# Odd mixer reordered: the first head pair ahead of v, pools among the later pairs, the output product to match; score products on all 128 rows

## The chip, the cores and the metric

One core of one Trainium2 chip runs the whole program. The metric is the device time of one execution in microseconds (us); several executions are timed and their median is given. The profile is one further execution taken by the hardware profiler. TensorE is written PE, its weight loads PEld, VectorE DVE, ScalarE ACT, GpSimd POOL and SyncE SP.

## The reference, cut to what matters

A trunk of two layers on 512 tokens of width 1024 in float32. Each layer is a SwiGLU block, a mixer and a SwiGLU block. The first (even) layer mixes with two recurrences; the second (odd) layer with attention and pooling. Only the odd mixer is touched:

```python
proj = h @ odd_w_in                       # 1024 -> q, k, v, u of 512 columns each
q, k, v, u = jnp.split(proj, [512, 1024, 1536], axis=-1)
y_c = _chunk_band_attention(q, k, v, ...) # 8 heads of 64; q and k normalized per head
y_d = _multiscale_pool(u, pool_w, scale)  # 4 groups of 128 channels, windows 2, 4, 8, 16
mixed = jnp.concatenate([y_c, y_d], axis=-1) @ odd_w_out
x = x + mixed
...
scores = einsum('bclhd,bckhd->bhclk', q, k) * 64**-0.5 + bias      # then softmax, then @ v
pooled = trailing_mean(u, w) - u;  y_d = (pooled @ pool_w[g]) * scale
```

## The kernel before, in words

The program is written down in one pass by a Python class that keeps an estimate of each engine's clock. Each engine executes its instructions in the order in which they were written, so the order is fixed at build time. There is a main stream of PE products; between its groups of products, generators ("threads": a norm, a pooling group, an attention block) emit their next instructions when the estimate says that an engine could start on them. Since one helper records every operation, all instructions carry one line in the profile (L203); they are told apart by the names of their tiles.

All large products are made in three passes for precision: an operand is split into an upper and a lower part (`fp32r`), and upper x upper, upper x lower and lower x upper are added up in PSUM. So a product of one 128 x 128 weight block with 128 x 512 of activations is a group of three PE instructions of 512 columns (`ps<-hg,whl`, or `ps<-whl,hg` for v). A weight unit (`raw`, 128 x 1024, 512 KB) is loaded by SP's DMA queue, and split into `whl` by an ACT cast and a DVE subtraction; the units that a table `BY_DMA` names (of `wod` those at places 8 to 11, of `wodo` the first four) get the lower part by two ACT operations and an adding DMA that POOL issues. Outside of the SwiGLU blocks three `whl` tiles rotate.

The odd mixer (function `odd`) runs in this order:

- v for all tokens: four units `wv`, each 24 instructions of PE, into four banks of PSUM; ACT scales them into `vt` (a `hg` tile).
- twelve units `wod` of 24 instructions each, in the order k0 q0 k1 q1 k2 q2 k3 q3 pool3 pool2 pool1 pool0, where k and q are of a pair of heads (128 columns). DVE multiplies each result by the rows' norm factors (`rsB`) on its way out of PSUM.
- after each q, a thread `qk_norm`: squares (`sqk`, ACT), their sums per head by 64 products of 2 columns in all (`ps<-hm,sqk`), a Newton square root on DVE (`rqv`, `rqt`, `rqy`), the factors spread by PE (`ps<-ident,rx`), and the split into `ks` (upper part over lower part, 128 rows), `qs` (upper part twice) and `ql` (lower part of q).
- attention blocks (`attn`, pair t, block qi of 128 queries), two at a time in the order of pairs: scores, on DVE bias and maximum (`s<-ps,rqy,strip`, `st<-s`), exponential on ACT, reciprocal and scaling on DVE, transposes on PE (`ps<-ident,s`), ACT copies (`pT`), products with v (`ps<-pT,hg`, each head into 64 rows of PSUM). The pair's result is split into a `hg` tile when its four blocks are done.
- pooling groups (`pool_g`): doubling sums on DVE (`pl`, `plo`), a product with `pw`, ACT and DVE to split it.
- the output product: eight units `wodo`, four for each half of the columns, in the order OUT_ORDER = 2, 3, 0, 1, where unit kp needs mixed tiles 2 kp and 2 kp + 1: kp 0 pairs 0 and 1, kp 1 pairs 2 and 3, kp 2 pools 0 and 1, kp 3 pools 2 and 3. The next SwiGLU block follows.

The score of a head is two PE instructions of N = 128 (qi + 1) columns: one that contracts all 128 rows of `qs` and `ks`, and one that contracts 64 rows, `ql` with the upper part in `ks`:

```python
nc.tensor.matmul(out=pss[hh][:, 0:N], lhsT=qs[:, hh, qc], rhs=ks[:, hh, 0:N], start=True, stop=False)
nc.tensor.matmul(out=pss[hh][:, 0:N], lhsT=ql[rows[hh], qc], rhs=ks[rows[hh], hh, 0:N], start=False, stop=True)
```

The functions that the diff touches:

Of the kernel before, what the change touches and what calls it, by code (L numbers as in the profile page):

```python
# [32 lines left out]
for _i in range(4):  # L33
    ODD_ORDER += [("k", _i, 512 + P * _i), ("q", _i, P * _i)]
ODD_ORDER += [("pool", _i, 1536 + P * _i) for _i in (3, 2, 1, 0)]
PRM = 2048
OUT_ORDER = [2, 3, 0, 1]
# FFN: quads of four weight units (gate and up of two column tiles) in groups; a group's down products run
# between the pairs of the next group
# [4 lines left out]
# tiles: of all phases, and more of them in the FFNs  # L44
# [42 lines left out]
def unit_plan(stages):  # L87
    plan = []
    for s in stages:
        if s == "even":  # L90
            plan += [("wev", n) for n in range(len(EVEN_ORDER))] + [("wglu", j) for j in range(2)]
            plan += [("wevo", cg, kp) for cg in range(2) for kp in OUT_ORDER]
        elif s == "odd":
            plan += [("wv", kp) for kp in range(4)] + [("wod", n) for n in range(len(ODD_ORDER))]
            plan += [("wodo", cg, kp) for cg in range(2) for kp in OUT_ORDER]
        elif s[0] == "f":
            plan += [k for k in ffn_items(int(s[1])) if k[0] != "blocks"]
    return plan
# [8 lines left out]
class Clock:  # L107
    """An estimate, while the program is written down, of when each engine gets to what it has been given."""
# [106 lines left out]
class Ring:  # L215
    """Tiles of one kind, counted: taken when they are made and given back with their last reader."""
# [31 lines left out]
class Builder:  # L248
# [31 lines left out]
    # generators that emit their parts in turn with the main stream of products  # L280
# [34 lines left out]
    # waits in a generator until an engine could start on these operands without holding up others  # L315
# [14 lines left out]
    # counted tiles: a place is taken before the tile is made and left with its last reader  # L330
# [23 lines left out]
    # banks of PSUM  # L354
# [78 lines left out]
    # products that nothing reads keep the tensor engine's clock up while it waits  # L433
# [6 lines left out]
    # the mixers' small parameters  # L440
# [33 lines left out]
    # weight units come in the order of the plan, loaded and split ahead of their products  # L474
# [95 lines left out]
    # the lower part as minus the upper one plus the weights themselves, added by the DMA  # L570
# [44 lines left out]
    # RMS norm: x times the gains, split, goes into the products, and the rows' factors come after them  # L615
# [46 lines left out]
    # what the norm left; its factors may come later  # L662
# [11 lines left out]
    # two units, so that there is work while the last parts of h come in  # L674
# [34 lines left out]
    # what waits for the norm's factors  # L709
# [7 lines left out]
    # one unit of an output product into four banks; the last one finishes the banks one by one  # L717
# [23 lines left out]
    # the FFN, its gate and up products in seven block products for eight (Strassen's scheme in Winograd's form):  # L741
    # the blocks are two column tiles by two halves of D (weights) and two halves of D by two of the tokens
# [83 lines left out]
    # the last output products begin: what they finish goes on to the next norm  # L826
# [23 lines left out]
    # x, normalized, as float32 (from the split parts when x has gone on)  # L850
# [15 lines left out]
    # sums of blocks of the normalized x  # L866
    def blocks(self, h, gi, late):
# [5 lines left out]
        # the last ones stay until they can go in place of h, the others are made again  # L873
# [29 lines left out]
        # the normalized x itself takes the place of what the unnormalized products read  # L903
# [29 lines left out]
    def pair(self, w, tag):  # L933
# [6 lines left out]
        # of two products in a bank, the one that is read first comes last: one engine at a time in a bank  # L940
# [30 lines left out]
    # up * silu(gate), split; how much of it is done: 1 the silu, 2 the product too  # L971
# [18 lines left out]
    # accurate functions on small tiles  # L990
# [51 lines left out]
    # parameters of the S5 mixer, per eighth of its groups, into DRAM scratch  # L1042
    def s5_prepare(self, pool):
# [100 lines left out]
        # powers of the unit phase: E, E^2, ... E^32  # L1144
# [6 lines left out]
        # the same for pairs of groups, one in each half of the partitions  # L1151
# [6 lines left out]
        # G, K and T0  # L1158
        def gains_of_outputs(e):
# [14 lines left out]
            # K and T0, a group in each quarter of the partitions  # L1174
# [23 lines left out]
        # B  # L1198
# [25 lines left out]
        # rotation tables and decay, for half of the groups  # L1224
# [96 lines left out]
    def s5_quarter(self, q, ys):  # L1321
# [13 lines left out]
        # 2*gelu(y), split  # L1335
# [82 lines left out]
    # SSD  # L1418
# [81 lines left out]
    # o <- 2*o*sigmoid(2*o), by a silu as long as the activation engine has its table, or else by a tanh  # L1500
# [241 lines left out]
    def qk_norm(self, t, kq):  # L1742
# [32 lines left out]
        # per head: key parts and query parts, one over the other, for the exact products  # L1775
# [5 lines left out]
        ql = p.tile([P, S], F32R, tag="ql", name=self.n("ql"), bufs=2)  # L1781
        half = [slice(0, 64), slice(64, 128)]
        for hh in range(2):
            me, other = half[hh], half[1 - hh]
            yield from self.on("ACT", qf)
            nc.scalar.copy(out=qs[me, hh], in_=qf[me])
            nc.scalar.copy(out=qs[other, hh], in_=qf[me])
            yield from self.on("ACT", kf)
            nc.scalar.copy(out=ks[me, hh], in_=kf[me])
            yield from self.on("DVE", qs)  # L1790
            v.tensor_tensor(out=ql[me], in0=qf[me], in1=qs[me, hh].bitcast(F32), op=ALU.subtract)
            yield from self.on("DVE", ks)
            v.tensor_tensor(out=ks[other, hh], in0=kf[me], in1=ks[me, hh].bitcast(F32), op=ALU.subtract)
# [3 lines left out]
    def attn(self, t, qi):  # L1797
# [12 lines left out]
        for hh in range(2):  # L1810
            nc.tensor.matmul(out=pss[hh][:, 0:N], lhsT=qs[:, hh, qc], rhs=ks[:, hh, 0:N], start=True, stop=False)
            nc.tensor.matmul(out=pss[hh][:, 0:N], lhsT=ql[rows[hh], qc], rhs=ks[rows[hh], hh, 0:N], start=False, stop=True)
# [96 lines left out]
    def odd(self, then):  # L1909
# [4 lines left out]
        with tc.tile_pool(name=self.n("odd"), bufs=2) as p:  # L1914
# [13 lines left out]
            # v, token-major  # L1928
            pv = [None] * 4
            for kp in range(4):  # L1930
                w = self.unit("wv", kp)
                for k2 in range(2):
                    k = 2 * kp + k2
                    cols = slice(k2 * 512, k2 * 512 + 512)
                    self.until(lambda: h[k] is not None)
                    for tb in range(4):
                        if pv[tb] is None:
                            pv[tb] = self.main_ps()
                        ts = slice(tb * P, tb * P + P)
                        nc.tensor.matmul(out=pv[tb], lhsT=h[k][:, 0, ts], rhs=w[:, 0, cols], start=k == 0, stop=False)  # L1940
                        nc.tensor.matmul(out=pv[tb], lhsT=h[k][:, 0, ts], rhs=w[:, 1, cols], start=False, stop=False)
                        nc.tensor.matmul(out=pv[tb], lhsT=h[k][:, 1, ts], rhs=w[:, 0, cols], start=False, stop=k == 7)
                        self.tick()
# [7 lines left out]
            self.until(self.scaled)  # L1951
            for tb in range(4):
# [4 lines left out]
            for n, (kind, i, _) in enumerate(ODD_ORDER):  # L1957
                w = self.unit("wod", n)
# [18 lines left out]
            for cg in range(2):  # L1977
                self.stream(("wodo",), self.mixed, OUT_ORDER, cg)
# [87 lines left out]
```

## Time and profile before

| | us |
|---|---|
| median of 3 runs | 1833.75 (1830.42 to 1837.24) |
| the profiled execution: its span, first to last instruction | 1837.6 |
| PE busy in it | 1819.0 |
| DVE busy | 1429.3 |
| ACT busy | 753.1 |

Busy time is the union of an engine's instructions; a PE instruction's end is modelled, so the PE's pace is better read from one start to the next. The profiled execution lies 3.85 us above the median. The odd mixer takes 1277.5 us to 1484.6 us of the span: its first v product starts at 1277.50, and the 192nd instruction of the output product ends its slot there.

### The profile page before, as it was taken

How to read it: one execution, taken by the hardware profiler on the slowest of the kernel's cores; microseconds unless marked ns; L12 is line 12 of the kernel's file. 1: busy time of each engine (PE TensorE's matmuls, PEld its weight loads, DVE VectorE, ACT ScalarE, POOL GpSimd, SP SyncE). 2: the span in 40 equal slices, each digit the busy share in tenths (PEclk: the TensorE clock that was granted, in tenths of full speed). 3: DMA queues.
4: the chain of work that ended last, by engine and by line, in shares of the span. 5: the costliest groups of instructions: out<-in, count | busy, mean ns of one | idle time of the engine just before them, and what ended most of it. 6: DMA issues, size and time to landing. Idle time of an engine off the chain costs nothing.

```text
span 1837.6 us, 26795 instructions
## 1 busy us (share of the span) xinstructions
PE 1819.0 (99%) x10514; PEld 1574.3 (86%) x10514; DVE 1429.3 (78%) x2599; ACT 753.1 (41%) x1082; POOL 16.6 (1%) x31
## 2 busy tenths in 40 slices
PE   9999999999999999999999999999999999999999
PEld 7877888978878899999888999998876788999997
DVE  8989868778986888877688988866477578988864
ACT  4224423333664444333344443334455444434331
POOL 0000000000000000000000000000000000000000
PEclk9999999999999999999999999999998999999999
DMA  5246432347772323333422243342334321333331
GB/s 197 93 132 196 143 103 69 115 145 209 186 195 79 93 81 115 104 104 104 138 69 77 96 117 103 103 138 88 102 81 92 92 81 58 120 109 105 104 104 69
DMA packets 80749, 207.16 MB, mean 113 GB/s; under 512 B 18000, under 2 KB 30320, under 8 KB 79472
## 3 DMA queue, kind: packets, MB, share of 16 engines
q1 hardware_dynamic: 78032, 196.52, 34.2%
q0 software_dynamic: 2448, 8.91, 2.9%
q8 instruction: 83, 1.36, 0.3%
q14 instruction: 42, 0.34, 0.1%
q10 hardware_dynamic: 144, 0.02, 0.0%
HBM read 192.82 MB, written 12.60 MB: 112 GB/s over the span
## 4 chain that ended last, share of the span: by engine, by line
PE 88%; DVE 9%; issue 1%; DMA 1%; ACT 1%; SPq 0%; DVEq 0%; ACTq 0%
PE ps L203 88%; DVE whl L203 1%; DVE hg L203 1%; DMA ssb<-acsd 1%; DVE s_t L203 1%; DVE us L203 1%; DVE ex L203 1%; DVE ssb L203 0%; DVE acc L203 0%; DVE s5x L203 0%; ACT whl L203 0%; DVE sc L203 0%; DMA hg<-s5us 0%; DVE s_sc L203 0%; DVE x L203 0%
## 5 line engine op out<-in xcount | busy, mean ns | idle before, releaser
L203 PE MATMUL ps<-hg,whl 128*128 128x512 f32 (+1 forms) x8688 | 1616.6, 346 | 6.6 <-DVE hg L203 2.7
L203 PEld LDWEIGHTS ps<-hg,whl 128*128 128x128 f32 x8688 | 1379.6, 190 | 209.3 <-DVE hg L203 4.9
L203 ACT CAST whl<-raw 128x1024 fp32r<-128x1024 f32 x366 | 382.3, 1050 | 544.3 <-PE ps L203 324.5
L203 DVE TENSOR_TENSOR whl<-raw,whl 128x1024 fp32r<-128x1024 f32 x349 | 423.5, 1220 | 185.3 <-ACT whl L203 184.6
L203 DVE SCALAR_TENSOR_TENSOR x<-ps,x 128x512 f32<-128x512 f32 x128 | 86.8, 685 | 37.1 <-PE ps L203 35.5
L203 DVE TENSOR_TENSOR raw<-raw,raw 128x512 f32<-128x512 f32 (+1 forms) x182 | 111.2, 648 | 2.2
L203 ACT CAST hg<-us 128x512 fp32r<-128x512 f32 x88 | 52.0, 618 | 105.3 <-DVE us L203 105.0
L203 PE MATMUL ps<-hg,wh 128*128 128x256 f32 x624 | 83.4, 283 | 0.0
L203 ACT ACTIVATE gs<-gs 128x1024 f32<-128x1024 f32 x44 | 46.6, 1059 | 85.4 <-DVE gs L203 85.4
L203 PEld LDWEIGHTS ps<-hg,wh 128*128 128x128 f32 x624 | 78.6, 192 | 0.0
L203 ACT COPY p<-ps 128x256 f32<-128x256 f32 x52 | 19.3, 371 | 96.0 <-PE ps L203 76.1
L203 DVE TENSOR_TENSOR raw<-raw 128x512 f32<-128x512 f32 (+1 forms) x78 | 46.4, 595 | 15.5 <-DMA raw<-in_wgu_dram 15.3
L203 DVE TENSOR_TENSOR hg<-us,hg 128x512 fp32r<-128x512 f32 x88 | 57.7, 682 | 0.0
L203 DVE TENSOR_TENSOR us<-gs,us 128x1024 f32<-128x1024 f32 x44 | 53.6, 1217 | 0.4
L203 ACT ACTIVATE hg<-x,gains 128x512 fp32r<-128x512 f32 x48 | 33.6, 720 | 33.2 <-DVE x L203 30.4
L203 ACT CAST hg<-raw 128x512 fp32r<-128x512 f32 x58 | 34.1, 618 | 22.2 <-DVE raw L203 21.6
L203 DVE TENSOR_TENSOR hg<-raw,hg 128x512 fp32r<-128x512 f32 x58 | 38.0, 683 | 0.1
L203 DVE SCALAR_TENSOR_TENSOR hg<-x,gains,hg 128x512 fp32r<-128x512 f32 x48 | 34.9, 743 | 2.7 <-ACT hg L203 2.7
L203 DVE TENSOR_TENSOR wh<-raw,wh 128x512 fp32r<-128x512 f32 x52 | 35.5, 683 | 0.0
L203 DVE TENSOR_TENSOR us<-ps,rsB 128x512 f32<-128x512 f32 x40 | 28.9, 721 | 4.6 <-PE ps L203 4.5
L203 ACT CAST wh<-raw 128x512 fp32r<-128x512 f32 x52 | 32.0, 616 | 0.0
L203 DVE TENSOR_TENSOR acc<-acc,sq 128x512 f32<-128x512 f32 x42 | 28.8, 685 | 0.9
(263 smaller groups left out, 1112.4 us busy)
## 6 DMA issues: line engine op xcount, KB each, us to landing
raw<-in_wgu_dram SPq DMA_DIRECT2D x176, 512.0 KB, 3.5
raw<-in_wdn_dram SPq DMA_DIRECT2D x88, 512.0 KB, 3.6
raw<-in_wev_dram SPq DMA_DIRECT2D x16, 512.0 KB, 3.7
prm<-prm SPq DMA_DIRECT2D x8, 1024.0 KB, 6.6
raw<-in_wod_dram SPq DMA_DIRECT2D x12, 512.0 KB, 3.4
raw<-in_wevo_dram SPq DMA_DIRECT2D x8, 512.0 KB, 6.3
raw<-in_wodo_dram SPq DMA_DIRECT2D x8, 512.0 KB, 6.5
x<-in_xT_dram SPq DMA_DIRECT2D x8, 256.0 KB, 5.2
```

Of the source, the lines that this page charges most:

```text
L203: r = f(*args, **kw)
```

## The change

The order of the odd mixer's units becomes k0 q0, then the four units of v, then k1 q1 pool3 k2 q2 pool2 k3 q3 pool1 pool0. The first two units go through `proj_tiles`, which the SwiGLU blocks use for theirs: four of the first unit's eight groups, four of the second's, then the rest in turn; both weight tiles are given back at the end. v goes into the other four banks of PSUM ("a"). The output product takes its units in the order 3, 0, 2, 1. `BY_DMA` is the same, so the units split with DMA are now k3, q3, pool1 and pool0. The lower part of q becomes a tile with 128 rows per head whose other 64 rows are zero, and the second score product contracts all 128 rows; two such tiles are made once, with four POOL memsets, and are used by turns. No product, DVE or ACT operation is added or taken away. (Comments are removed too.)

```diff
 ODD_ORDER = []
-for _i in range(4):
+for _i, _pools in enumerate(((),(3,),(2,),(1,0))):
     ODD_ORDER += [("k", _i, 512 + P * _i), ("q", _i, P * _i)]
-ODD_ORDER += [("pool", _i, 1536 + P * _i) for _i in (3, 2, 1, 0)]
+    ODD_ORDER += [("pool", _j, 1536 + P * _j) for _j in _pools]
...
+ODD_OUT = [3,0,2,1]
...
-            plan += [("wv", kp) for kp in range(4)] + [("wod", n) for n in range(len(ODD_ORDER))]
-            plan += [("wodo", cg, kp) for cg in range(2) for kp in OUT_ORDER]
+            plan += [("wod", n) for n in range(2)] + [("wv", kp) for kp in range(4)]
+            plan += [("wod", n) for n in range(2, len(ODD_ORDER))]
+            plan += [("wodo", cg, kp) for cg in range(2) for kp in ODD_OUT]
...
-        ql = p.tile([P, S], F32R, tag="ql", name=self.n("ql"), bufs=2)
+        ql = self.qls[t % 2]
...
-            v.tensor_tensor(out=ql[me], in0=qf[me], in1=qs[me, hh].bitcast(F32), op=ALU.subtract)
+            v.tensor_tensor(out=ql[me, hh], in0=qf[me], in1=qs[me, hh].bitcast(F32), op=ALU.subtract)
...
-            nc.tensor.matmul(out=pss[hh][:, 0:N], lhsT=ql[rows[hh], qc], rhs=ks[rows[hh], hh, 0:N], start=False, stop=True)
+            nc.tensor.matmul(out=pss[hh][:, 0:N], lhsT=ql[:, hh, qc], rhs=ks[:, hh, 0:N], start=False, stop=True)
...
+            self.qls = [p.tile([P, 2, S], F32R, name=f"ql{i}", bufs=1) for i in range(2)]
+            for ql in self.qls:
+                nc.gpsimd.memset(ql[64:128, 0].bitcast(F32), 0.0)
+                nc.gpsimd.memset(ql[0:64, 1].bitcast(F32), 0.0)
+            self.wait_room("hg")
+            kq = self.slot()
+            self.sideb = 4
+
+            def first(pss, kq):
+                for i, ps in enumerate(pss):
+                    self.evac_rs(ps, kq[:, i])
+                    self.free(ps)
+                self.sideb = 2
+                self.add("qk_norm", self.qk_norm(0, kq))
+
+            pss = self.proj_tiles([("wod", 0), ("wod", 1)], h)
+            self.put(lambda kq=kq: first(pss, kq))
...
-                            pv[tb] = self.main_ps()
+                            pv[tb] = self.main_ps("a")
...
             for n, (kind, i, _) in enumerate(ODD_ORDER):
+                if n < 2:
+                    continue
...
-                self.stream(("wodo",), self.mixed, OUT_ORDER, cg)
+                self.stream(("wodo",), self.mixed, ODD_OUT, cg)
```

What moves, on three places of two engines. PE at the start of the mixer, before: the first v unit, of which each row is three products of one token block (`hg_11794`, `hg_11804` are the first two parts of h).

```order
L203 MATMUL ps_11926<-whl_11837,hg_11794 128x512 x3
L203 MATMUL ps_11938<-whl_11837,hg_11794 128x512 x3
L203 MATMUL ps_11944<-whl_11837,hg_11794 128x512 x3
L203 MATMUL ps_11950<-whl_11837,hg_11794 128x512 x3
L203 MATMUL ps_11926<-whl_11837,hg_11804 128x512 x3
```

Where the second unit ends now: the last groups of k0 (`ps_11933`) and q0 (`ps_11961`) in turn, the spread of the norm factors (`rqy`), v's first four groups, then the first pair's sums of squares (`hm`).

```order
L205 MATMUL ps_11933<-hg_11938,whl_11837 128x512 x3
L205 MATMUL ps_12015<-ident,rqy_11991 128x128 x4
L205 MATMUL ps_11961<-hg_11938,whl_11874 128x512 x3
L205 MATMUL ps_12027<-whl_11942,hg_11794 128x512 x3
L205 MATMUL ps_12036<-whl_11942,hg_11794 128x512 x3
L205 MATMUL ps_12044<-whl_11942,hg_11794 128x512 x3
L205 MATMUL ps_12051<-whl_11942,hg_11794 128x512 x3
L205 MATMUL ps_12057<-hm,sqk_12034 128x2
```

The two units take the first 16 groups of three, and v follows. The first pair's squares, which stood in the middle of k1, stand after v's fourth group, and its first scores one group after v's last product (before: one group after q1). PE where the projections end and the output product begins, before: the last pool's product (`plo`), the first output group, which reads that pool's result `hg_13151`, and pair 3's first scores (`hg_12833`, `hg_12834`, `ql_12835`).

```order
L203 MATMUL ps_13149<-plo_13121,pw 128x512
L203 MATMUL ps_13154<-hg_13151,whl_12925 128x512 x3
L203 MATMUL ps_13163<-hg_12833,hg_12834 128x128
L203 MATMUL ps_13163<-hg_12833,ql_12835 128x128
L203 MATMUL ps_13164<-hg_12833,hg_12834 128x128
L203 MATMUL ps_13164<-hg_12833,ql_12835 128x128
```

The same place now: the last projection group (`ps_13074`), pair 3's first two blocks of scores, the first output group.

```order
L205 MATMUL ps_13074<-hg_11938,whl_12872 128x512 x3
L205 MATMUL ps_13165<-hg_13088,hg_13089 128x128
L205 MATMUL ps_13165<-hg_13088,ql_11927 128x128
L205 MATMUL ps_13166<-hg_13088,hg_13089 128x128
L205 MATMUL ps_13166<-hg_13088,ql_11927 128x128
L205 MATMUL ps_13178<-hg_13088,hg_13089 128x256
L205 MATMUL ps_13178<-hg_13088,ql_11927 128x256
L205 MATMUL ps_13179<-hg_13088,hg_13089 128x256
L205 MATMUL ps_13179<-hg_13088,ql_11927 128x256
L205 MATMUL ps_13194<-hg_12855,whl_12948 128x512 x3
```

The scores are ahead of the output product, whose first group reads pool 2's result `hg_12855`; that pool's product stands in the unit k3, three units earlier. The last pool's product now stands after nine output groups, seven groups ahead of the first that reads its result. DVE in pair 1's attention, now (`s_12565` and `s_12578` are its first two blocks' scores for one head, `pl` pool 3's doubling sums).

```order
L205 SCALAR_TENSOR_TENSOR s_12579<-ps_12573,rqy_12438,strip_12150 128x256
L205 TENSOR_REDUCE st_12580<-s_12579 128x1
L205 TENSOR_TENSOR pl_12542<-pl_12525 128x508
L205 COPY pl_12542<-pl_12525 128x4
L205 RECIPROCAL st_12567<-st_12567 128x2
L205 TENSOR_SCALAR s_12565<-s_12565,st_12567 128x128
```

Before, DVE's first pooling operation stood behind all of pair 1's scores. From the start of the last SwiGLU block on, the engines' orders are the same as before.

## Rows read from the trace of the kernel before

**Rows 1.** The page: span, busy time of each engine, and in 40 slices of 46 us the granted clock of PE in tenths.

```profile
span 1837.6 us, 26795 instructions
PE 1819.0 (99%) x10514; PEld 1574.3 (86%) x10514; DVE 1429.3 (78%) x2599; ACT 753.1 (41%) x1082; POOL 16.6 (1%) x31
PEclk9999999999999999999999999999998999999999
```

**Rows 2.** The odd mixer in stretches: from:to, length, then busy time of PE, PEld, DVE, ACT and POOL (instructions), granted clock of PE, busy share of the DMA engines, GB/s.

```profile
1277.50:1301.10 23.60, 23.60 (x113) 19.81 (x112) 11.78 (x24) 9.09 (x13) 1.16 (x8) 1.00 0.58 190
1301.10:1326.40 25.30, 25.30 (x125) 21.27 (x123) 13.16 (x25) 10.15 (x15) 0.00 (x0) 1.00 0.27 84
1326.40:1373.30 46.90, 46.90 (x266) 36.60 (x264) 34.31 (x88) 30.85 (x67) 2.67 (x3) 1.00 0.37 86
1373.30:1383.60 10.30, 10.30 (x32) 7.14 (x32) 6.62 (x20) 1.41 (x3) 0.00 (x0) 0.50 0.07 20
1383.60:1411.70 28.10, 28.10 (x155) 20.58 (x154) 22.61 (x58) 17.95 (x39) 2.54 (x3) 1.00 0.53 113
1411.70:1432.00 20.30, 17.88 (x56) 10.41 (x56) 9.92 (x22) 7.16 (x15) 0.86 (x1) 0.58 0.24 53
```

**Rows 3.** Timeline of PE, score products at full clock: start, duration, what it writes and reads, contracted rows * weight columns, shape. `ps<-hg,hg` contracts 128 rows, `ps<-hg,ql` 64.

```profile
1355.36 0.30 PE L203 MATMUL ps<-hg,hg 128*128 128x128 f32 x1
1355.59 0.32 PE L203 MATMUL ps<-hg,ql 64*128 64x128 f32 x1
1356.35 1.66 PE L203 MATMUL ps<-hg,whl 128*128 128x512 f32 x6
1360.59 0.36 PE L203 MATMUL ps<-hg,hg 128*128 128x256 f32 x1
1361.82 0.50 PE L203 MATMUL ps<-hg,whl 128*128 128x512 f32 x1
1339.09 0.44 PE L203 MATMUL ps<-hg,hg 128*128 128x384 f32 x1
1340.56 0.96 PE L203 MATMUL ps<-hg,whl 128*128 128x512 f32 x3
1341.36 0.40 PE L203 MATMUL ps<-hg,hg 128*128 128x512 f32 x1
1342.97 0.50 PE L203 MATMUL ps<-hg,whl 128*128 128x512 f32 x1
```

**Rows 4.** Groups of PE instructions by shape in 1200 to 1276 us (the SwiGLU block before): count, busy time, mean ns of one (instructions overlap, so busy time by count is the pace).

```profile
L203 PE MATMUL ps<-hg,whl 128*128 128x512 f32 x203 | 46.7, 389 | 0.0
L203 PE MATMUL ps<-hg,whl 128*128 128x256 f32 x216 | 26.4, 283 | 0.0
```

**Rows 5.** Timeline of PE around the first fall of the clock.

```profile
1371.46 0.96 PE L203 MATMUL ps<-hg,whl 128*128 128x512 f32 x3
1372.26 2.40 PE L203 MATMUL ps<-hm,sqk 128*128 128x2 f32 x16
1375.64 0.80 PE L203 MATMUL ps<-hg,hg 128*128 128x512 f32 x1
1378.54 7.43 PE L203 MATMUL ps<-hg,whl 128*128 128x512 f32 x21
1385.81 0.38 PE L203 MATMUL ps<-ident,rx 128*128 128x128 f32 x2
```

**Rows 6.** Timeline of PE at the second fall and the start of the output product; in brackets the idle time before an instruction and who ended it.

```profile
1411.67 0.88 PE L203 MATMUL ps<-ident,s 128*128 128x128 f32 x6
1414.19 1.99 PE L203 MATMUL ps<-plo,pw 128*128 128x512 f32 x2 [1.64 <-DVE pl L203]
1423.03 2.01 PE L203 MATMUL ps<-hg,whl 128*128 128x512 f32 x3 [0.78 <-ACT hg L203]
1431.82 1.09 PE L203 MATMUL ps<-pT,hg 128*64 128x128 f32 x16
1457.93 0.50 PE L203 MATMUL ps<-hg,whl 128*128 128x512 f32 x1 [0.69 <-ACT hg L203]
```

**Rows 7.** Groups of DVE instructions by shape in 1326 to 1458 us: count, busy time, mean ns of one, idle time before them. `s<-ps,rqy,strip`, `st<-s` and `s<-s,st` are the three steps of an attention block; `hg<-ps,psc,hg` is a pool's split.

```profile
L203 DVE SCALAR_TENSOR_TENSOR s<-ps,rqy,strip 128x512 f32<-128x512 f32 x8 | 6.0, 750 | 3.1 <-PE ps L203 3.0
L203 DVE TENSOR_REDUCE st<-s 128x1 f32<-128x512 f32 x8 | 5.5, 686 | 0.3
L203 DVE SCALAR_TENSOR_TENSOR s<-ps,rqy,strip 128x384 f32<-128x384 f32 x8 | 4.9, 613 | 7.6 <-PE ps L203 7.6
L203 DVE TENSOR_REDUCE st<-s 128x1 f32<-128x384 f32 x8 | 4.4, 553 | 0.3
L203 DVE TENSOR_SCALAR s<-s,st 128x512 f32<-128x512 f32 x8 | 3.5, 483 | 0.1
L203 DVE TENSOR_SCALAR s<-s,st 128x384 f32<-128x384 f32 x8 | 3.0, 418 | 0.1
L203 DVE SCALAR_TENSOR_TENSOR hg<-ps,psc,hg 128x512 fp32r<-128x512 f32 x4 | 3.0, 745 | 2.1 <-ACT hg L203 2.1
L203 DVE TENSOR_TENSOR whl<-raw,whl 128x1024 fp32r<-128x1024 f32 x4 | 4.9, 1222 | 4.5 <-ACT whl L203 4.4
```

**Rows 8.** DVE at the start of the mixer (timeline: the split of the last part of h), and POOL's memsets in 1270 to 1330 us (a group: count, busy time, mean ns of one).

```profile
1282.47 0.74 DVE L203 SCALAR_TENSOR_TENSOR hg<-x,gains,hg 128x512 fp32r<-128x512 f32 x1
L203 POOL MEMSET strip<- 64x64 f32 x8 | 1.2, 144 | 748.1 <-DVE acc L203 740.8 <-DMA strip<-in_strip_dram 7.3
```

More of the change, by code (lines that the diff above doesn't have):

```diff
@@ L1935, in odd @@
                     self.until(lambda: h[k] is not None)
+                    if self.later and self.scaled():
+                        self.put(lambda: None)
                     for tb in range(4):
                         if pv[tb] is None:
-                            pv[tb] = self.main_ps()
+                            pv[tb] = self.main_ps("a")
                         ts = slice(tb * P, tb * P + P)
@@ L1951, in odd @@
             self.until(self.scaled)
+            self.put(lambda: None)
             for tb in range(4):
```

## The prediction

> **What bounds the kernel now.** The page comes first. PE is busy 1819.0 of 1837.6 us, and the clock's digits show 9 in every slice of 46 us but one, the thirty-second [rows 1]. So PE sets the time, and what an edit is worth is what it takes out of PE's own stream or out of PE's waits. The one digit below 9 lies in the odd mixer, which is all that the change touches, so the second view is that mixer by stretches. It shows full clock except from 1373.30 to 1383.60 (0.50) and around 1411.70 to 1432.00 (0.58); PE is idle almost only in the second of these (17.88 us busy of 20.30) [rows 2]. DVE is well filled but not full, 34.31 of 46.90 us and 22.61 of 28.10 us [rows 2]. The third view is PE's timeline, read from start to start, since a record's end overlaps the next record. It gives the pace of score products [rows 3], the two falls of the clock [rows 5, 6] and PE's three idle gaps above half a us: 1.64 us for a pool's DVE sums, 0.78 us for the pool that the output product reads first, 0.69 us for pair 3's result [rows 6].
>
> **Part one: score products on 128 rows.** A block's four products alternate 128, 64, 128, 64 rows. From the first to what follows the fourth they take 0.99 us at 128 columns (1355.36 to 1356.35), 1.23 at 256 (1360.59 to 1361.82), 1.47 at 384 (1339.09 to 1340.56) and 1.61 at 512 (1341.36 to 1342.97) [rows 3]: 5.30 us for a pair of heads, 21.2 for four. The same columns in products that all contract 128 rows go by at 46.7 / 203 = 0.230 us for 512 and 26.4 / 216 = 0.122 for 256 [rows 4]. So 128 columns cost between 0.06 (a quarter of 512) and 0.122, 384 about 0.17. I take 0.12 for 128, since 256 already lies above half of 512: 4 x (0.12 + 0.122 + 0.17 + 0.23) = 2.57 us a pair, 10.3 for four. Gain 10.9, up to 11.9 with the low price of 128 columns, and nothing if the spacing has another cause (a rival below). The extra time is about 0.13 to 0.22 us on each product at any width, which looks like the array emptying at each change of height: the weight block can't be brought in behind the product before it.
> The Trainium skill (TensorEngine Tiling (Array Packing), section Key Properties) says that changing the tiling mode drains TensorE; these rows agree with 0.25 us for 128 columns where 0.12 or less is due [rows 3, 4]. The same page speaks against the change in When to Use Tiling: with a contraction of 64 or less, two row tiles may run side by side, so filling up with zeros throws away up to a factor of two. In these rows no two 64-row products stand next to each other, so nothing of that is had now; by that rule the better edit would be another order, and this one would bring less than the 10.9.
> The four memsets of the zero halves go to POOL ahead of the `strip` memsets. A 64 x 64 one takes 0.144 us [rows 8]; 512 columns cost from 0.14 to 1.2 each, 4.6 us in all at most, behind the same release of memory, about 1280. The first score product comes after 49 groups of 0.69 us, 34 us into the mixer, so this is hidden; without that cover it would be 4.6 us once.
>
> **Part two: k0 and q0 ahead of v.** PE's work is the same. The two units take the same first two places in the load order as two v units did. h is now used up faster: its last part is needed after 14 groups of 0.69 us, 1277.5 + 9.7 = 1287.2; its split ends at 1283.21 [rows 8], so no wait. Both weight tiles are held for 16 groups, so v's second unit can be split only then: one operation on ACT and one on DVE, the latter 1.22 us [rows 7], against eight groups, 5.5 us, of v's first unit. Nothing, even at twice that. v's banks of PSUM are the ones that the block before has just given back. What is gained: pair 0's norm and splits run under v, where DVE was busy 11.78 of 23.60 us [rows 2], and the attention blocks begin one group after v.
>
> **Part three: pools among the pairs, output order 3, 0, 2, 1.** The first output group reads pool 2, whose product is three units old, so the waits of 1.64 and 0.78 us at 1414 and 1423 have no cause any more [rows 6]. Pair 3's scores start ahead of the output product, and seven groups, 4.8 us, stand between its last product with v and the group that needs its result; the 0.69 at 1457.93 [rows 6] goes.
> The stretch 1411.67 to 1431.82 took 20.15 us [rows 6]. At full clock and without waits its work is: 12 output products 12 x 0.23 = 2.8, the eight scores 1.61 + 0.99 = 2.6, four passes for two pools 0.9, 14 transposes and 12 passes with v about 2.3, and 0.3 for changes between them: 8.9 us. Lost: 11.2 us. Ahead of the fall PE had transposed 128 columns at a time and then stood idle 1.64 us.
> The first fall, at 1373.3, followed a run of narrow work: one group, then sixteen passes of two columns [rows 5]. From 1378.54 to 1385.81, 21 products took 7.27 us where 4.83 are due; the 512-column scores before them 2.90 where 1.61 are due; of the narrow products ahead, 2.3 us (1373.30 to 1375.64) ran at half clock, which costs half of it, 1.2. Lost: 4.9 us. That place changes: fewer narrow products, no 64-row ones, pair 1's 512-column scores followed by full groups. I count the fall as gone; it is the least certain term.
>
> **What is given back.** DVE's instructions are the same, but they crowd. From 1301.1 to 1432.0 DVE was busy 13.16 + 34.31 + 6.62 + 22.61 + 9.92 = 86.6 us of 130.9, 66% [rows 2]. Of this about 12 us now lie under v: four weight splits of 1.22 and pair 0's norm, ten operations of up to 512 columns at about 0.69 by the nearest row (686 ns) [rows 7], small ones included; the other 75 us stand beside the ten units k1 to pool 0, which PE does in 85 us (240 products at 0.23, three pairs' scores 7.7, and about 22 of transposes, v, norm and pool products): 88%. The densest place is k2 to k3, where pair 1's blocks, pair 2's norm and pools 3 and 2 meet. In before the densest row without a wait of PE on DVE was 22.61 / 28.10 = 80% [rows 2]; held to that, 75 us would need 94, so waits lie between 0 and 9 us. A place worked by hand: from pair 3's 384-column scores to their transposes PE has one pool product (two passes), eight groups and the 512-column scores, 0.46 + 5.52 + 0.92 = 6.9 us; DVE has in that time 2 x (0.613 + 0.553), 2 x (0.750 + 0.686), a pool's 0.745, and a reciprocal and 2 x 0.418, in sum 6.9 us, and 1.1 more for the 512 columns, which PE wants 0.6 later [rows 7]. About half a us of wait there. I take 4 us for some eight such places, nearer to zero since the order leaves PE most of its groups between a block's steps. What queues behind such a wait is the main stream itself.
>
> **The sum.** Scores 10.9, second fall and its waits 11.2, first fall 4.9, end of pair 3 0.7: 27.7; less 4: about 24 us. The profiled span of 1837.6 becomes about 1814; it lies 3.85 above the median of the runs, so the median goes from 1833.75 to 1810.
>
> **Rivals.**
> *The clock falls once more.* Sixteen two-column products and 28 passes with v, transposes between them, now stand close together in pool 3's unit. For: such a mix preceded both falls. Against: a like mix from 1355.36 on [rows 3] did not cause one, the clock was 1.00 up to 1373.30 [rows 2]. At half clock half of the time is lost; by the two falls' lengths, 10.3 and some 17 us, that is 5 to 8.5: gain 15 to 19, 1817.
> *DVE becomes the bound.* Waits of 9 us or more between k1 and pool 0, perhaps with a fall: gain 10, 1824. It decides once DVE's share there must stay at 80%.
> *The 128-row scores gain nothing*, because the spacing comes from the change of PSUM bank between heads. Against: the second product of a head stays in its bank and still takes 0.25 at 128 columns [rows 3]. Gain 13, 1821.
> *Slower.* PE waits on DVE in each block of pairs 1 and 2, narrow products and idle gaps alternate, and PE stays at half clock through the ten units. Half clock costs half of its time; 27.7 us of expected gains and 9 more are used up once about 74 us are spent at half clock, against 27 now; then 1843 or more. Only a stretch as poor as 1411 to 1432 did this so far, and it had two idle gaps.
>
> **How the numbers follow.** Forecast as above, gain 19 to 28: 0.56. One more fall: 0.19. DVE the bound: 0.12. Scores gain nothing: 0.08. Slower: 0.05. Half a per cent, 9.2 us, is about what a measurement of this kernel can tell from no change. Above it lie the first, second and fourth case and some of the third: faster 0.86; within it most of the rest of the third: same 0.10; slower 0.04. The range runs from a gain of 30 (no waits, cheap 128 columns, the change-over costs of the 64-row products gone too) to 10, where DVE's bound begins: 1804 to 1824.
>
> **What would show it.** Right: a block's four scores take about 0.5 us at 128 and 0.9 at 512 columns; no idle PE at the first output group; the clock at 1.00 from 1373 on; the span of the mixer 183 instead of 207. Wrong: score products still 0.25 apart or more at 128 columns; PE ended by DVE `s`, `plo` or `rx` between k1 and pool 0; a stretch at 0.50 among the pairs.

## The result and the profile after

The changed kernel takes 1812.51 us (median of 4 runs, 1810.71 to 1813.25); the kernel before, on the same chip, 1833.45 us. The ratio is 0.989 [0.986, 0.991]: 1.1% faster, clear of the noise, and 2.5 us above the forecast of 1810.

The page of the kernel after, with the rows that answer to [rows 1]:

```profile
span 1808.7 us, 26795 instructions
PE 1792.4 (99%) x10514; PEld 1564.3 (86%) x10514; DVE 1428.9 (79%) x2599; ACT 754.7 (42%) x1082; POOL 18.7 (1%) x35
PEclk9999999999999999999999999999999999999999
```

The 8 in the clock's digits is gone. The odd mixer after in stretches, as in [rows 2] (k0 and q0; v; the pairs; the change to the output product; the output product):

```profile
1274.17:1297.80 23.63, 23.63 (x125) 20.20 (x124) 16.39 (x40) 9.61 (x15) 3.25 (x12) 1.00 0.54 169
1297.80:1330.00 32.20, 32.20 (x158) 26.12 (x157) 18.56 (x36) 17.21 (x34) 0.00 (x0) 1.00 0.27 82
1330.00:1380.00 50.00, 50.00 (x312) 41.37 (x311) 41.93 (x110) 32.47 (x68) 3.46 (x4) 1.00 0.43 100
1380.00:1403.00 23.00, 23.00 (x151) 18.58 (x150) 17.69 (x44) 16.31 (x30) 1.71 (x2) 1.00 0.46 106
1403.00:1409.00 6.00, 4.74 (x20) 3.25 (x19) 5.77 (x17) 2.66 (x9) 0.86 (x1) 1.00 0.71 151
1409.00:1455.70 46.70, 46.70 (x243) 38.10 (x242) 25.02 (x39) 22.22 (x38) 0.85 (x1) 1.00 0.43 127
```

The clock is 1.00 throughout, and PE is idle only in the six microseconds from 1403. The mixer takes 181.5 us (1274.17 to 1455.70) where it took 207.1 (1277.50 to 1484.6); the forecast was 183. The other 3.3 us between the two spans lie ahead of it, in code that did not change: the execution before had one more short half-clock stretch there, around 540, and a longer one from 100 to 110 (a clock of 0.66 there, 0.83 after).

Score products of pair 0 after, beside [rows 3] (PE's timeline; the second product of each head now contracts 128 rows):

```profile
1312.16 0.22 PE L205 MATMUL ps<-hg,hg 128*128 128x128 f32 x1
1312.22 0.28 PE L205 MATMUL ps<-hg,ql 128*128 128x128 f32 x1
1312.56 0.91 PE L205 MATMUL ps<-hg,whl 128*128 128x512 f32 x3
1313.30 0.28 PE L205 MATMUL ps<-hg,hg 128*128 128x256 f32 x1
1313.77 4.95 PE L205 MATMUL ps<-hg,whl 128*128 128x512 f32 x21
1320.64 0.45 PE L205 MATMUL ps<-hg,hg 128*128 128x384 f32 x1
1321.45 0.85 PE L205 MATMUL ps<-hg,whl 128*128 128x512 f32 x3
1324.65 0.50 PE L205 MATMUL ps<-hg,hg 128*128 128x512 f32 x1
1325.69 1.54 PE L205 MATMUL ps<-hg,whl 128*128 128x512 f32 x6
```

A block takes 0.40, 0.47, 0.81 and 1.04 us where it took 0.99, 1.23, 1.47 and 1.61 [rows 3]: 2.72 instead of 5.30 for a pair, 10.3 less for four.

The start of the output product after, beside [rows 6] (PE's timeline, idle time in brackets):

```profile
1402.56 1.55 PE L205 MATMUL ps<-hg,whl 128*128 128x512 f32 x6
1404.62 0.97 PE L205 MATMUL ps<-hg,whl 128*128 128x512 f32 x3 [0.52 <-DVE s L205]
1406.34 3.02 PE L205 MATMUL ps<-hg,whl 128*128 128x512 f32 x12 [0.74 <-DVE pu L205]
```

The first two output groups start without a wait. The third and the fourth wait 0.52 and 0.74 us until DVE has read a score block and the last projection: by the order for banks of PSUM, not for operands (the last experiment tries this). These are all of PE's waits above 0.2 us in this mixer.

### The profile page after: what moved, and what is told of

Read it like the earlier page. It is cut to its first block, busy times and chain, and to the rows that moved or that the text cites. A ratio compares the mean times of both kernels' runs of the same rounds, so it can differ in the third digit from the quotient of the medians.

```text
span 1808.7 us, 26795 instructions
## 1 busy us (share of the span) xinstructions
PE 1792.4 (99%) x10514; PEld 1564.3 (86%) x10514; DVE 1428.9 (79%) x2599; ACT 754.7 (42%) x1082; POOL 18.7 (1%) x35
## 4 chain that ended last, share of the span: by engine, by line
PE 88%; DVE 8%; DMA 2%; issue 1%; ACT 1%; SPq 0%; DVEq 0%; ACTq 0%
PE ps L205 88%; DVE whl L205 1%; DVE hg L205 1%; DVE us L205 1%; DVE ex L205 1%; DVE ssb L205 1%; DMA raw<-in_wglu_dram 0%; DMA prm<-prm 0%; DMA s5ys<-ys 0%; ACT whl L205 0%; DVE s5x L205 0%; DMA ssb<-acsd 0%; DVE sc L205 0%; ACT hg L205 0%; DMA raw<-in_wgu_dram 0%
```

## The experiments

The clock falls to half for some microseconds in some executions of one and the same program, so each kernel's times are given beside the mean granted clock of its runs. Time x (1 - clock) is an estimate of what an execution lost to the falls, since a fall reads 0.50 [rows 2] and products in it take nearly twice their time (a block of 512-column scores 2.90 us [rows 5] against 1.61 [rows 3]); the rest is called its time at full clock. A run's clock is given to three digits, which is 0.9 us either way, so only means are used. "Before" was timed again on each chip. In us:

| kernel | runs | median | mean | mean clock | lost to the clock | at full clock |
|---|---|---|---|---|---|---|
| before, first chip | 17 | 1830.04 | 1831.08 | 0.9958 | 7.8 | 1823.3 |
| scores_only | 6 | 1815.60 | 1816.19 | 0.9978 | 3.9 | 1812.3 |
| order_only | 12 | 1826.10 | 1825.48 | 0.9968 | 5.8 | 1819.7 |
| side_by_side | 6 | 1817.46 | 1816.91 | 0.9977 | 4.2 | 1812.7 |
| before, second chip | 21 | 1829.87 | 1831.17 | 0.9957 | 7.9 | 1823.3 |
| after_again | 6 | 1812.05 | 1811.76 | 0.9983 | 3.0 | 1808.7 |
| pools_last | 12 | 1824.32 | 1823.79 | 0.9952 | 8.7 | 1815.1 |
| out_order | 10 | 1823.37 | 1823.06 | 0.9961 | 7.1 | 1816.0 |
| banks | 6 | 1812.49 | 1813.26 | 0.9978 | 3.9 | 1809.3 |
| before, third chip | 9 | 1830.34 | 1830.28 | 0.9967 | 6.1 | 1824.2 |
| v_first | 5 | 1815.10 | 1814.17 | 0.9986 | 2.5 | 1811.6 |

The theory was that of the prediction: cheaper score products, two falls of the clock with their waits taken away, some waits on DVE given back. The rivals were that the falls have another cause than the order, that the zeros waste what packed 64-row products could have, and that parts of the order do nothing or harm.

**The kernel before, once more.** No edit.

> The kernel before once more, unchanged, for a second profile. If the two falls of PE's clock in the odd mixer belong to its order of work, they come again at the same products (a pair's sums of squares ahead of pair 1's 512-column scores, and the last pools), and the mixer takes 205 to 209 us. If they depend on the execution, one or both are missing or elsewhere, and the mixer takes 195 to 203 us; then part of what the first profile lost to them is no gain of the change.

The mixer by stretches, cut at the falls of this execution, in the columns of [rows 2]:

```profile
1376.70:1383.50 6.80, 6.80 (x15) 4.76 (x16) 5.26 (x14) 1.19 (x2) 0.00 (x0) 0.50 0.00 1
1383.50:1412.00 28.50, 28.50 (x160) 21.03 (x158) 23.20 (x59) 18.19 (x39) 2.54 (x3) 1.00 0.50 111
1412.00:1428.00 16.00, 13.29 (x42) 7.39 (x40) 9.17 (x22) 5.59 (x12) 0.86 (x1) 0.68 0.29 68
```

The waits of 1.64 and 0.78 us stood where they stood in [rows 6], but the falls were shorter: 6.8 + 10.2 us at half clock (0.32 / 0.5 of 16.00) against some 27 in the profile that the prediction read. The time, 1837.28, is among the longest of this kernel; the other 17 executions, at a mean clock of 0.9958 against 0.992 here, lost less still. The mixer took 203.4 us, between the two sides. In these two profiles the place of the falls repeats and their length does not.

**The changed kernel, once more.** No edit; on one chip with pools_last, out_order and banks.

> The changed kernel once more, on the same chip as the three below. Theory, that the clock falls of the mixer come with the 64-row score products: the granted clock is 1.00 from the first k0 product to the end of the output product in this profile too, and the times stay within 3 us of 1812.5, with every execution's mean clock at 0.997 or above. Rival, that the profile after was merely a lucky execution: a fall of 3 to 10 us somewhere in the mixer, and times spread up to 1820, as the kernel before spreads from 1826.7 to 1837.3.

1812.05 us, ratio 0.990 [0.987, 0.992]; the clock was 1.00 from 1230 to 1530 in this profile too, with the same two waits, 0.52 and 0.75. The times run from 1809.24 to 1813.45, one of them 3.3 below 1812.5, at clocks of 0.997 to 1.000. The first profile after was no lucky one.

**The 128-row scores alone.** The order of before; `ql` as in the changed kernel:

```diff
-matmul(out=pss[hh][:, 0:N], lhsT=ql[rows[hh], qc], rhs=ks[rows[hh], hh, 0:N], ...)
+matmul(out=pss[hh][:, 0:N], lhsT=ql[:, hh, qc], rhs=ks[:, hh, 0:N], ...)
```

> Order of before, only the lower score product on 128 rows with zeros. Theory (each change between 128 and 64 rows costs 0.13 to 0.22 us): the four scores of a block go from 0.99, 1.23, 1.47, 1.61 us to about 0.46, 0.48, 0.68, 0.92, gain 10 to 12 us while the waits for the pools and the second fall of the clock stay. Rival (the 64-row products also bring the falls about): the clock stays at 1.00 through the mixer and the gain is 15 to 20 us. Rival (the spacing has another cause): no gain, and scores as far apart as before.

1815.60 us, ratio 0.992 [0.990, 0.993]. Its timeline of PE at the output product, and the stretch of both former falls:

```profile
1403.62 1.12 PE L203 MATMUL ps<-plo,pw 128*128 128x512 f32 x2 [1.64 <-ACT pT L203]
1408.31 0.50 PE L203 MATMUL ps<-hg,whl 128*128 128x512 f32 x1 [0.78 <-ACT hg L203]
1409.46 0.73 PE L203 MATMUL ps<-hg,whl 128*128 128x512 f32 x2 [0.65 <-DVE hg L203]
1437.28 0.49 PE L203 MATMUL ps<-hg,whl 128*128 128x512 f32 x1 [0.69 <-ACT hg L203]
```

```profile
1370.00:1440.00 70.00, 66.01 (x397) 50.70 (x397) 53.23 (x130) 39.66 (x86) 4.28 (x5) 1.00 0.41 99
```

The scores of pair 0 take 0.39, 0.52, 0.82 and 0.92 us a block, as the theory had it. All the waits of before are there, and the clock is 1.00 in this execution, as the first rival had it. So these waits alone did not bring a fall here. The medians differ by 14.4 us, more than the theory's 10 to 12: at full clock the edit is worth 1823.3 - 1812.3 = 11.0 us, and 3.9 more are no longer lost to the clock.

**The order alone.** The changed kernel with the 64-row products of before (the diff above, reversed).

> Order of the changed kernel, scores as before (64 rows of the lower part). Theory: scores as far apart as before, no wait at the first output products for a pool, gain 8 to 13 us, that is what is left of 21 us after the scores' 11. Rival (scores gain nothing): the whole 20 to 22 us. Rival (the clock falls are the 64-row products' doing): falls come in the new order too and the gain is under 8 us.

1826.10 us, ratio 0.997 [0.996, 0.998]. Its one wait in the mixer, and the mixer as one stretch, both of the profiled execution, the fastest of the twelve:

```profile
1415.80 3.02 PE L205 MATMUL ps<-hg,whl 128*128 128x512 f32 x12 [0.32 <-DVE pu L205]
1270.00:1465.00 195.00, 194.68 (x1016) 152.12 (x1015) 127.91 (x285) 101.58 (x192) 7.98 (x16) 1.00 0.41 109
```

The median is 3.9 us lower, less than the theory's 8 to 13 and within the last rival's bound of 8. At full clock the order is worth 3.6 us. That is about what its waits were: 1.64, 0.78 and 0.69 [rows 6] with the short ones beside them make 3.3 us in the first profile and 3.6 in before_again; 0.32 is left. But the mean execution lost 5.8 us to the clock against 3.0 in after_again, so with 64-row products the clock still fell in other executions, though the waits were gone; where, this profile does not show. The two parts add up: 11.0 + 3.6 = 14.6 at full clock, and after_again stands 14.6 below before.

**64-row products side by side.** The order of after, 64-row products; the two of a block's heads, on rows 0 to 63 and 64 to 127, follow one another:

```diff
 for hh in range(2):
     matmul(..., lhsT=qs[:, hh, qc], rhs=ks[:, hh, 0:N], start=True, stop=False)
+for hh in range(2):
     matmul(..., lhsT=ql[rows[hh], qc], rhs=ks[rows[hh], hh, 0:N], start=False, stop=True)
```

> Order of the changed kernel, scores with 64 rows, but in a block both 128-row products first and then both 64-row products, one on rows 0 to 63 and one on rows 64 to 127, in two banks. So the height changes twice in a block instead of four times. By the rule that row tiles run side by side the two small products take the time of one: a 512-column block 0.9 to 1.0 us as with zeros (0.92), and the time is that of the changed kernel within 2 us. If they do not run side by side: 512 columns 1.15 to 1.3 us a block, and 4 to 7 us more than the changed kernel.

1817.46 us, ratio 0.993 [0.991, 0.994]. Two blocks of pair 0 on PE's timeline, and for comparison a 64-row product of order_only with the product behind it (the last two rows):

```profile
1313.70 0.33 PE L205 MATMUL ps<-hg,hg 128*128 128x128 f32 x2
1313.97 0.33 PE L205 MATMUL ps<-hg,ql 64*128 64x128 f32 x2
1314.23 0.96 PE L205 MATMUL ps<-hg,whl 128*128 128x512 f32 x3
1326.89 0.73 PE L205 MATMUL ps<-hg,hg 128*128 128x512 f32 x2
1327.55 0.50 PE L205 MATMUL ps<-hg,ql 64*128 64x512 f32 x2
1327.98 2.37 PE L205 MATMUL ps<-hg,whl 128*128 128x512 f32 x9
1328.00 0.50 PE L205 MATMUL ps<-hg,ql 64*128 64x512 f32 x1
1328.43 0.49 PE L205 MATMUL ps<-hg,hg 128*128 128x512 f32 x1
```

Both 64-row products of 512 columns together take 0.43 us, where one such product took 0.43 by itself in order_only: they run at the same time. Yet a block takes 0.53 and 1.09 us, with zeros 0.40 and 1.04. The 1.09 lies between the two sides of the expectation, and the time, 5.4 us above after_again, is that of the side without overlap. The two changes of height that are left cost more than the overlap gives. The blocks of a pair take 0.46 us more than with zeros, some 1.8 for four pairs, of the 4.0 between the two kernels at full clock; the rest was not traced. The Trainium skill (TensorEngine Tiling (Array Packing), section When to Use Tiling) lists a contraction of 64 as a case for twofold row tiling. The trace agrees with the overlap, and shows no gain by it with two products between changes.

This execution also shows a fall with no wait of PE ahead of it. It comes in the same sequence as the first fall in [rows 5]: sixteen products of two columns, eight with v, 512-column scores.

```profile
1391.00:1394.40 3.40, 3.40 (x9) 2.46 (x8) 3.19 (x11) 0.00 (x0) 0.00 (x0) 0.50 0.23 71
```

**Pools last, the first pair early.** The changed kernel with

```diff
-for _i, _pools in enumerate(((),(3,),(2,),(1,0))):
+for _i, _pools in enumerate(((),(),(),(3,2,1,0))):
-ODD_OUT = [3,0,2,1]
+ODD_OUT = [2,3,0,1]
```

> The first pair ahead of v and the 128-row scores, but the four pools last and the output order 2, 3, 0, 1 as before: part two with part one, without part three. Theory, that of the order's 3 to 5 us nearly all are PE's waits for pools and for pair 3's result: the waits at the start of the output product come back (1.6 and 0.8 us, or more, since attention has less left to fill with), and the time is that of the 128-row scores alone, 1815.6, give or take 1.5. Rival, that the early first pair is what brings the order's part, by spreading DVE's work: 1812 to 1813, no wait above half a us at the output product.

1824.32 us, ratio 0.996 [0.995, 0.997]: 8.7 above the scores alone, which neither side had expected. Its waits (PE's timeline) and the stretch behind the first:

```profile
1407.50 0.43 PE L205 MATMUL ps<-ident,s 128*128 128x128 f32 x2 [2.83 <-DVE s L205]
1418.66 0.49 PE L205 MATMUL ps<-hg,whl 128*128 128x512 f32 x1 [0.78 <-ACT hg L205]
1421.02 0.73 PE L205 MATMUL ps<-hg,whl 128*128 128x512 f32 x2 [1.86 <-DVE hg L205]
```

```profile
1409.10:1416.00 6.90, 5.87 (x19) 3.13 (x20) 5.69 (x15) 1.99 (x6) 0.00 (x0) 0.51 0.50 133
```

With the first pair early, attention is further on when the projections end, and the pools' DVE work stands there with too little of PE's to cover it: 2.83 us of waiting, then 6.9 us at half clock, with no 64-row score product in the program. With three short ones of 0.52 to 0.53 between the first and the second row its waits add up to 7.0 us, against 4.0 in scores_only. The means show where the time goes: 2.8 us more than scores_only at full clock, and 4.8 more lost to the clock.

**The output order of before.** The changed kernel with `ODD_OUT = [2,3,0,1]` alone.

> The changed kernel with the output product in the order 2, 3, 0, 1, so that its first groups read pools 0 and 1, whose units have just ended. Theory, that the output order must match the place of the pools: PE waits at the first output group for pool 1 and pool 0, about as long as a pool's DVE sums with its two splits take, 2 to 6 us in all; 1815 to 1818. Rival, that the 128-row scores of pair 3 and the transposes fill that time: 1812 to 1813, no wait above half a us.

1823.37 us, ratio 0.995 [0.994, 0.997]: the one line is worth 11.3 us against after_again, more than expected. Waits and the first stretch at half clock:

```profile
1409.69 1.30 PE L205 MATMUL ps<-ident,s 128*128 128x128 f32 x4 [4.00 <-DVE s L205]
1416.27 1.13 PE L205 MATMUL ps<-plo,pw 128*128 128x512 f32 x2 [0.86 <-DVE plo L205]
1420.55 1.12 PE L205 MATMUL ps<-hg,whl 128*128 128x512 f32 x2 [1.88 <-DVE hg L205]
```

```profile
1410.40:1413.60 3.20, 3.20 (x14) 2.11 (x16) 1.47 (x5) 0.92 (x3) 0.00 (x0) 0.51 0.64 178
```

PE cannot start the output product, since its first group reads a pool whose sums are not made, and it stands 4.00 us at the transposes of pair 3. With 0.78 for the pool's split (a row between these) the waits come to 7.5 us instead of 1.3; the clock takes about four more on average.

**v first, pools among the pairs.** The scores alone, with the pools' places and the output order of after.

> The order of before up to q1, with v first, but pools 3 and 2 among the later pairs, the output order 3, 0, 2, 1 and the 128-row scores: part three with part one, without part two. It completes a square of four: with v first and pools last 1815.6, with the first pair early and pools last 1824.3, with both 1812. Theory, that pools among the pairs need the early first pair, since otherwise attention is one pair late and pair 3's result is wanted by the output product (its second unit) before it is there: PE waits for pair 3 and for the blocks ahead of it, several us in all at 1410 to 1430, 1819 to 1825. Rival, that the place of the pools is good by itself and the early pair worth nothing: 1811 to 1813, no wait above 1 us.

1815.10 us, ratio 0.991 [0.990, 0.993]. The waits at the output product's end of attention:

```profile
1427.88 1.25 PE L204 MATMUL ps<-pT,hg 128*64 128x128 f32 x12 [0.29 <-ACT pT L204]
1430.62 1.57 PE L204 MATMUL ps<-pT,hg 128*64 128x128 f32 x16 [0.27 <-ACT pT L204]
1432.88 0.49 PE L204 MATMUL ps<-hg,whl 128*128 128x512 f32 x1 [0.68 <-ACT hg L204]
```

Neither side was right: little is lost and little won. The square of four medians is 1815.6 (v first, pools last), 1815.1 (v first, pools among), 1824.3 (pair early, pools last) and 1812.1 (both). So an early first pair costs 8.7 with the pools last, most of it through the clock, and gives about 3 with them among the pairs, where the ranges overlap (1811.65 to 1815.90 and 1809.24 to 1813.45). The four stood on three chips; against the kernel before on its own chip each gains, at full clock, 11.0, 12.6, 8.2 and 14.6 us, so there the early pair costs 2.8 or gives 2.0.

**Other banks for the output product.** The changed kernel with the output product in the "a" banks and what runs beside it in "b".

```diff
-            self.sideb = 0
+            self.sideb, self.sidea = 4, 0
-                self.stream(("wodo",), self.mixed, ODD_OUT, cg)
+                self.stream(("wodo",), self.mixed, ODD_OUT, cg, "a")
```

> The changed kernel with the output product in the other four banks of PSUM, and the attention blocks and pools that are left beside it in the four that the projections had. Theory, that the waits of 0.52 and 0.74 us at the third and fourth output group are waits for a bank that a score block and the last projection still hold: both are gone, and the time is 1 to 1.3 us lower than that of the changed kernel. Rival, that they only move, to the side work that now shares four banks: the waits come back at a score block or a transpose, and the time is the same or up to 2 us longer.

1812.49 us against 1812.05 for the changed kernel on the same chip: the same, as the rival had it. The one wait left:

```profile
1409.18 3.01 PE L205 MATMUL ps<-hg,whl 128*128 128x512 f32 x12 [0.90 <-DVE hg L205]
```

The waits of 0.52 and 0.74 are gone, and the fourth group waits 0.90 for a DVE write that stands behind two score blocks, the split of pool 1's result. That this too is a bank, held by pool 1's product, is read from the order only; it wasn't tried. No version was found that beats the changed kernel.

## Why the prediction held, point by point

- **PE sets the time.** Right. At full clock what could be traced of the gain is PE's own pace and PE's waits.
- **Scores, 10.9.** Right: 10.3 by the rows and 11.0 by the runs at full clock. The block of 128 columns takes 0.40, so 128 columns cost some 0.11, near the 0.12 that was taken. At 384 and 512 the first product of a block, which stands behind products with v, costs 0.28 and 0.34 instead of 0.17 and 0.23; this was left out. That the time went into emptying the array is the prediction's guess; the runs show only that it goes when the heights are equal. The rival of the PSUM banks falls: products of two heads in two banks go by at 0.11 to 0.12 us each.
- **The rule of the Trainium skill against the change** (TensorEngine Tiling (Array Packing), section When to Use Tiling). The trace agrees that two 64-row products overlap, and not that this order would be the better one: side_by_side is 5.4 us slower than after_again by the medians, 4.0 at full clock.
- **Part two, no cost.** Right for its loads, splits and banks: PE is busy 23.63 of 23.63 us. What failed is that it was priced apart from part three. With the pools last it costs 8.7 us, 2.8 of them at full clock.
- **Part three, the waits at the output product.** Right: 1.64, 0.78 and 0.69 are gone, and out_order shows that with the pools among the pairs they don't go without the output order. Worth 3.6 at full clock, short waits included.
- **The two falls, 11.2 and 4.9.** The step that failed, in two ways. Less the waits of 1.64 and 0.78 they were booked at 13.7 us. For the profiled execution that was right: some 27.4 us at half clock, 0.8 of them idle, cost 13.3. But its clock of 0.990 lies below the 0.991 to 0.999 of 21 others. By the runs' clocks the kernel before loses 7.9 us to falls in all its stages and the changed one 3.0, so the mean gain is about 5; and of the falls outside the mixer, near 100, 420 and 540 us, some come and some stay out from profile to profile, in code that no run changed. The sum was carried from the profiled execution to the median as it stood. And the cause was laid to the waits and the narrow work. The 128-row products by themselves take the mean loss from 7.8 to 3.9 with the waits left in, the order by itself only to 5.8 with the waits gone. The fall in the sequence of two-column products and 512-column scores, with no wait ahead of it, stands in three of the four profiles with 64-row products (not in order_only) and in none of the five with 128-row products that have this sequence. That speaks for the 64-row products there; with so few executions it does not prove it. Pools_last and out_order show that a longer wait, 2.83 or 4.00 us, is followed by half clock without any 64-row score. So both can bring a fall, and which products or gaps it takes stays open.
- **Given back to DVE, 4.** Too much: 1.26, at another place and, by the order, for banks. In the pairs DVE is busy 41.93 of 50.00 us, 84%, with PE busy 50.00; the 80% that the bound rested on was merely the fullest stretch that the kernel before happened to have.
- **The sum.** Between the two profiled executions the mixer gained 25.6 us: 10.3 for the scores, 2.1 of waits (3.3 before, 1.3 after) and 13.3 for the falls make 25.7. The 24 were 10.9 + 3.1 + 13.7 - 4. Between the mean runs it is 11.0 + 3.6 + 4.8 = 19.4, and 20.9 between the first medians: less of the falls. So at full clock the forecast had 10.0 where 14.6 was measured, and for the falls 13.7 where the mean has 4.8. One error is 4.6 too low, 2.7 of it from what was given back to DVE, the other 8.9 too high; that they cancel in part, which leaves the forecast 2.5 us from the first median, is luck. Of the 14.6 the rows account for about 12.5; the last 2 were not traced (the time at full clock of single runs of the kernel before spreads by 1.2, as a standard deviation). The 3.85 us between the profiled execution and the median set a span against device times; in the later runs of this kernel the device time is 2.2 us above the span, so that execution was about 6 us longer than the median. The forecast does not hang on it, since it is the median less 24.
- **The rivals.** No fall in the mixer after, so not the first; DVE is not the bound; the scores gained all they should; nothing slower. But the mechanism of the slower rival, an idle gap and then half clock, is real: it shows where the early pair is made without the pools' new places, or without the output order.

## What to carry to other kernels

On a kernel that PE bounds, count changes of contraction height in the stream: filling a 64-row operand with zeros was worth 11 us at full clock here, three times what the whole reordering brought. Moves in a hand-made order are to be priced as a set, since each decides what covers the other's stalls: by the medians the same move cost 8.7 us or gave 3, at full clock it cost 2.8 or gave 2. And a stretch at half clock in one profile is to be taken at its average over executions, which the clock of each timed run gives.

## What the runs showed of the hardware

- Two 64-row products on the two halves of the rows run at the same time, 0.43 us for both at 512 columns, but a change of height costs about 0.13 to 0.2 us in each direction, so that here, with one such pair between changes, zeros were cheaper (0.40 against 0.53 us a block at 128 columns, 1.04 against 1.09 at 512).
- The granted clock differs between executions of one program on one chip: 0.991 to 0.999 over 21 runs of the kernel before, 1826.34 to 1840.79 us. With time x (1 - clock) taken off, 4.6 us of that spread of 14.5 are left.
